# A third of the weight chunks split by an accumulating DMA in place of GpSimd arithmetic

## Chip, cores and metric

The kernel runs on one core of a Trainium2 chip, in one launch. The metric is the device time of that launch in microseconds; the time before is the median of three runs.

## The reference

A small decoder trunk over 512 tokens of width 1024, batch 1, in float32: one retention layer with four heads, then one multi-head latent attention layer with sixteen heads. Each has a SiLU gate, an output projection and a post-norm:

```
x = LN(alpha*x + retention_layer(x, a_w_in, a_w_out))
k_nope, k_rope, v = shared_latent_kv(x, kv_w_down, kv_norm, kv_w_up)
x = LN(alpha*x + mla_layer(x, b_w_in, q_norm, w_uq, b_w_out, k_nope, k_rope, v))
```

All work of weight is matrix products of activations (512 rows) with weights that are read once from HBM.

## The kernel before

**Three products for one.** TensorE multiplies float32r values. Each operand is split into a high part (`hi`, the value cast to float32r) and a low part (`lo`, the value less its high part), and `mm3` (L95) adds three products in a PSUM bank: high by high, and the two of a high with a low part (L97 to L99). So every weight chunk needs both parts before TensorE can finish with it.

**Weights.** All weights come as chunks of 128 rows and at most 1024 columns (512 KB), in the order in which they are used. That order is the list `order` in `trunk_kernel`. The class `Weights` (L37) works through it: `issue` (L51) loads a chunk from HBM into a stage buffer `wst` by a DMA on SyncE's queue, lets ScalarE cast it to `whi` (L66), and lets VectorE or GpSimd subtract `whi` from `wst` into `wlo` (L67, L68). One chunk in three goes to GpSimd: those with `n % 3 == 2`, after the first seven, whose names are not in `on_vector` (L44). `get` (L72) hands a chunk to TensorE and keeps two more issued ahead. High and low parts have four buffers each (pool `wpt`), so the cast of a chunk waits until TensorE has finished with the chunk four places earlier; stage buffers are eight in the retention layer and two in the second.

**Chunks made in place.** Per retention head, values and gates are computed by seven block products (`p1` to `p7`, fourteen chunks, `w_vg` at L110) in place of eight. Some of their weights are sums or differences of weight blocks, made in the stage buffers by VectorE or, for heads 1 to 3, by GpSimd (L118). Such a chunk is given as a function (`callable`) and not as an array in HBM.

**Order.** The recording layer orders the instructions of each engine itself when the program is built; each engine then works its queue strictly in that order and waits for semaphores. GpSimd's queue also has small reciprocal roots (`rsqrt`, L254 to L258) that the normalisations wait for.

**Stages.** Head by head: values and gates, the retention scores and their products (`inner`), transposes, output projection (`o0` to `o3`). After head 3 come the shared latent (`lat`), the query latent (`ql0`, `ql1`), then for sixteen heads in eight pairs the chunks `gb` (gate), `k`, `q`, `r` (rotary queries), `vb` (values) and `bo` (output), between which the attention work stands. One chunk of 1024 columns keeps TensorE busy for 24 products of 512 columns.

Of the kernel before, what the change touches and what calls it, by code (L numbers as in the profile page):

```python
# [8 lines left out]
F32 = mybir.dt.float32  # L9
BF16 = mybir.dt.bfloat16  # L10
F32R = mybir.dt.float32r
AF = mybir.ActivationFunctionType
ALU = mybir.AluOpType
# [15 lines left out]
EAGER = 7  # L29
# [7 lines left out]
class Weights:  # L37
# [13 lines left out]
    def issue(self, between=None):  # L51


        nc = self.nc
        name, aps, n = self.todo.pop(0)
        st = aps() if callable(aps) else self.stage.tile([P, WC], F32, tag="wst", name="wst")
        pool, th, tl = self.place[name].pop(0) if self.place.get(name) else (self.parts, "whi", "wlo")
        hi = pool.tile([P, WC], F32R, tag=th, name="whi")
        lo = pool.tile([P, WC], F32R, tag=tl, name="wlo")
        for j, ap in enumerate(aps if isinstance(aps, list) else [aps]):  # L60
            sl = slice(j * n, (j + 1) * n)
            if j and between:
                between()
            if not callable(ap):
                self.last = nc.sync.dma_start(st[:, sl], ap)
            nc.scalar.copy(hi[:, sl], st[:, sl])  # L66
            eng = nc.gpsimd if self.n % 3 == 2 and self.n > EAGER and name not in self.on_vector else nc.vector  # L67
            eng.tensor_tensor(out=lo[:, sl], in0=st[:, sl], in1=hi.bitcast(F32)[:, sl], op=ALU.subtract)  # L68
        self.n += 1
        self.ready.append((name, hi, lo))  # L70

# [1007 lines left out]
```

## Time and profile before

| | |
|---|---|
| median of the runs | 935.09 us (934.62 to 936.39) |
| the profiled execution | 934.96 us, of it span 933.2 us |
| TensorE busy | 914.1 us, 98% of the span |
| VectorE busy | 646.2 us, 69% |
| ScalarE busy | 357.2 us, 38% |
| GpSimd busy | 176.9 us, 19% |
| low parts on VectorE (L68) | 132 + 2, 1243 ns in the mean of the 132 |
| low parts on GpSimd (L68) | 49, 2264 ns in the mean |
| casts of weights on ScalarE (L66) | 181 + 2, 964 ns in the mean of the 181 |
| moved by DMA | 97.45 MB, 104 GB/s in the mean |

How to read it: busy time is the union of an engine's instructions, and products of TensorE overlap in it, so 98% does not mean that it works at its best rate; whether it waits is read from the gaps between the starts of its products. An engine that is busy for less than the span costs time only where another waits for it. DMA issues are not counted as busy time of the engine that issues them.

### The profile page before, as it was taken

To read this page: it belongs to the slowest core of one execution; us is meant where nothing else is said; L and a number is where in the kernel's file an instruction comes from. 1 tells how busy PE (TensorE), PEld (TensorE's weight loads), DVE (VectorE), ACT (ScalarE), POOL (GpSimd) and SP (SyncE) were. 2 spreads that over 40 slices of the span, in tenths; PEclk is the share of its full clock that TensorE was granted. 3 is DMA by queue.
4 is the path that set the end of the run, shared out by engine and by line. 5 is a ranking of instruction groups with operands and counts; after the bars stand their busy time and mean duration, and the time that the engine had idled before them with its cause. 6 is when DMAs were issued, how large, how long until landed. Compare 5 with 4: busy or idle time off the path is not lost.

```text
span 933.2 us, 11971 instructions
## 1 busy us (share of the span) xinstructions
PE 914.1 (98%) x4553; PEld 774.7 (83%) x4553; DVE 646.2 (69%) x1117; ACT 357.2 (38%) x600; POOL 176.9 (19%) x108
## 2 busy tenths in 40 slices
PE   9979999999999999999999999999999999999996
PEld 6758888888888887888988888888888888888885
DVE  7998767967696779963377576464864738657577
ACT  6453334333433345132535343333433334334431
POOL 0001126221641160112312011010011021111204
PEclk9989999999999999999999999999999999999998
DMA  9164204520352051234134424242242422423222
GB/s 333 61 224 138 90 12 141 175 78 25 136 180 72 30 187 40 68 87 136 52 116 108 121 76 118 75 126 72 74 122 76 125 68 74 127 78 107 91 68 91
DMA packets 32362, 97.45 MB, mean 104 GB/s; under 512 B 4272, under 2 KB 4912, under 8 KB 32304
## 3 DMA queue, kind: packets, MB, share of 16 engines
q1 hardware_dynamic: 28800, 87.11, 28.6%
q10 hardware_dynamic: 3504, 9.57, 4.1%
q8 instruction: 36, 0.59, 0.3%
q14 instruction: 22, 0.18, 0.1%
HBM read 86.18 MB, written 2.10 MB: 95 GB/s over the span
## 4 chain that ended last, share of the span: by engine, by line
PE 82%; DVE 8%; issue 4%; POOL 3%; DMA 2%; ACT 0%; SPq 0%; DVEq 0%; POOLq 0%; ACTq 0%
PE ps L98 26%; PE ps L99 26%; PE ps L97 25%; DVE wlo L68 2%; PE ps L839 2%; POOL wst L118 1%; PE ps L816 1%; PE ps L817 1%; DMA wst<-in_w_g 1%; DMA r<-in_xT 1%; DVE wst L118 1%; PE ps L531 1%; POOL wlo L68 1%; DMA cosA<-in_cosA 1%; PE ps L298 1%
## 5 line engine op out<-in xcount | busy, mean ns | idle before, releaser
L66 ACT CAST whi<-wst 128x1024 fp32r<-128x1024 f32 (+3 forms) x181 | 173.1, 964 | 266.7 <-PE ps L98 94.8
L68 DVE TENSOR_TENSOR wlo<-wst,whi 128x1024 fp32r<-128x1024 f32 (+2 forms) x132 | 163.5, 1243 | 98.6 <-ACT whi L66 98.3
L68 POOL TENSOR_TENSOR wlo<-wst,whi 128x1024 fp32r<-128x1024 f32 (+3 forms) x49 | 110.9, 2264 | 621.4 <-ACT whi L66 591.4
L824 ACT ACTIVATE p<-ps,sm 128x512 f32<-128x512 f32 (+1 forms) x64 | 33.4, 526 | 66.6 <-DVE sm L821 66.5
L97 PE MATMUL ps<-qlt_h,whi 128*128 128x512 f32 x144 | 56.9, 395 | 0.0
L98 PE MATMUL ps<-qlt_l,whi 128*128 128x512 f32 x144 | 56.5, 392 | 0.0
L99 PE MATMUL ps<-qlt_h,wlo 128*128 128x512 f32 x144 | 56.3, 391 | 0.0
L97 PE MATMUL ps<-x1h,whi 128*128 128x512 f32 x128 | 50.6, 395 | 0.0
L97 PE MATMUL ps<-whi,oTh 128*128 128x512 f32 x128 | 50.2, 392 | 0.0
L99 PE MATMUL ps<-whi,oTl 128*128 128x512 f32 x128 | 50.0, 390 | 0.1
L98 PE MATMUL ps<-x1l,whi 128*128 128x512 f32 x128 | 50.0, 391 | 0.0
L99 PE MATMUL ps<-x1h,wlo 128*128 128x512 f32 x128 | 49.9, 390 | 0.0
L98 PE MATMUL ps<-wlo,oTh 128*128 128x512 f32 x128 | 49.8, 389 | 0.0
L97 PE MATMUL ps<-whi,ogh 128*128 128x512 f32 (+1 forms) x114 | 44.7, 392 | 0.0
L99 PE MATMUL ps<-whi,ogl 128*128 128x512 f32 (+1 forms) x114 | 44.1, 387 | 0.0
L98 PE MATMUL ps<-wlo,ogh 128*128 128x512 f32 (+1 forms) x114 | 44.0, 386 | 0.0
L890 DVE TENSOR_TENSOR r<-r,ps 128x512 f32<-128x512 f32 (+1 forms) x49 | 32.4, 671 | 10.4 <-PE ps L99 10.4
L97 PE MATMUL ps<-xTh,whi 128*128 128x512 f32 x96 | 37.6, 392 | 0.0
L98 PE MATMUL ps<-wlo,xTh 128*128 128x512 f32 x96 | 37.5, 390 | 0.1
L99 PE MATMUL ps<-xTh,wlo 128*128 128x512 f32 x96 | 37.4, 389 | 0.0
L98 PE MATMUL ps<-xTl,whi 128*128 128x512 f32 x96 | 37.4, 389 | 0.0
L97 PE MATMUL ps<-whi,xTh 128*128 128x512 f32 x96 | 37.4, 389 | 0.0
(248 smaller groups left out, 2394.0 us busy)
## 6 DMA issues: line engine op xcount, KB each, us to landing
wst<-in_w_g SPq DMA_DIRECT2D x22, 512.0 KB, 3.3
wst<-in_w_v SPq DMA_DIRECT2D x16, 512.0 KB, 3.4
wst<-in_w_ao SPq DMA_DIRECT2D x16, 512.0 KB, 3.9
wst<-in_w_gb SPq DMA_DIRECT2D x16, 512.0 KB, 3.8
qr<-uv ACTq DMA_DIRECT2D x64, 128.0 KB, 2.4
wst<-in_w_bo SPq DMA_DIRECT2D x16, 512.0 KB, 3.6
wst<-in_w_qk SPq DMA_DIRECT2D x12, 512.0 KB, 3.9
wst<-in_w_q SPq DMA_DIRECT2D x16, 384.0 KB, 3.1
```

Source lines behind the costliest of these rows:

```text
L66: nc.scalar.copy(hi[:, sl], st[:, sl])
L68: eng.tensor_tensor(out=lo[:, sl], in0=st[:, sl], in1=hi.bitcast(F32)[:, sl], op=ALU.subtract)
L97: nc.tensor.matmul(ps, lhsT=lh, rhs=rh, start=start, stop=False)
L98: nc.tensor.matmul(ps, lhsT=lh, rhs=rl, start=False, stop=False)
L99: nc.tensor.matmul(ps, lhsT=ll, rhs=rh, start=False, stop=stop)
L118: eng.tensor_tensor(out=out, in0=x, in1=y, op=ALU.subtract)
L298: nc.tensor.transpose(out=ps[:, k * P : (k + 1) * P], in_=src[:, k * P : (k + 1) * P], identity=ident)
L531: nc.tensor.transpose(out=ps[:, k * P : (k + 1) * P], in_=gs[h][:, n, k * P : (k + 1) * P], identity=ident)
L816: nc.tensor.matmul(ps, lhsT=rh[:, qs], rhs=krp[:, :n], start=False, stop=False)
L824: nc.scalar.activation(pp, ps, AF.Exp, bias=sm[:, qb, 1:2], scale=SCALE_B, accum_out=sm[:, qb, 2:3])
L839: nc.tensor.transpose(out=ps[:, do : do + P], in_=pr[i][:, so : so + P], identity=ident)
L890: nc.vector.tensor_tensor(out=dst, in0=dst, in1=ps, op=ALU.add)
```

## The change

For chunks that are loaded from an array in HBM and that the rule gives to GpSimd, ScalarE now writes the negative of the high part into `wlo`, and a DMA issued from GpSimd's queue adds the chunk, read from HBM a second time, to what stands there. The load into the stage buffer stays, for the cast. Chunks made in place that GpSimd split before are split by VectorE.

```diff
-            eng = nc.gpsimd if self.n % 3 == 2 and self.n > EAGER and name not in self.on_vector else nc.vector
-            eng.tensor_tensor(out=lo[:, sl], in0=st[:, sl], in1=hi.bitcast(F32)[:, sl], op=ALU.subtract)
+            if self.n % 3 == 2 and self.n > EAGER and name not in self.on_vector and not callable(ap):
+
+                low = lo[:, sl]
+                nc.scalar.activation(low, hi.bitcast(F32)[:, sl], AF.Copy, scale=-1.0)
+                nc.gpsimd.dma_start(low, ap, accum_op=ALU.add)
+            else:
+                nc.vector.tensor_tensor(out=lo[:, sl], in0=st[:, sl], in1=hi.bitcast(F32)[:, sl], op=ALU.subtract)
```

Lines after the edit stand five further down in the changed kernel: L97 to L99 become L102 to L104, L118 becomes L123, L258 becomes L263. The copy is L70, the DMA L71, the subtraction L73. In the built program GpSimd has 37 such DMAs and no low part, ScalarE 37 copies more, VectorE 146 subtractions in place of 134.

The recording layer also orders some instructions anew. On GpSimd, in head 3 of the retention layer, the queue before was, from a chunk of head 2's output projection on (`wst<-wst` are the differences made in the stage buffers, `o_rs` the reciprocal roots):

```order
L68 TENSOR_TENSOR wlo<-wst,whi 128x1024 x3
L118 TENSOR_TENSOR wst<-wst 128x1024 x3
L68 TENSOR_TENSOR wlo<-wst,whi 128x1024
L118 TENSOR_TENSOR wst<-wst 128x1024
L258 TENSOR_TENSOR o_rs<-rs_t,mhalf 128x1 x4
```

and in the changed kernel it is:

```order
L71 DMA wlo<-in_w_ao 128x1024
L123 TENSOR_TENSOR wst<-wst 128x1024 x4
L263 TENSOR_TENSOR o_rs<-rs_t,mhalf 128x1 x4
```

Of the three low parts before the first difference one is now a DMA, the other two and the one before the last difference have gone to VectorE.

On TensorE, at the first chunk of `ql0` (`x1h`, `x1l` are the parts of the layer's input, `ident,latn` the transposes of the latent), before:

```order
L298 MATMUL ps<-ident,latn 128x128 x4
L97 MATMUL ps<-whi,x1h 128x512
L98 MATMUL ps<-wlo,x1h 128x512
L99 MATMUL ps<-whi,x1l 128x512
L97 MATMUL ps<-whi,x1h 128x512
```

and now:

```order
L303 MATMUL ps<-ident,latn 128x128 x4
L102 MATMUL ps<-whi,x1h 128x512 x4
L303 MATMUL ps<-ident,latn 128x128 x2
L103 MATMUL ps<-wlo,x1h 128x512
L104 MATMUL ps<-whi,x1l 128x512
```

Three more products with the high part and two transposes stand ahead of the first product with the low part.

On TensorE, at the second `gb` chunk, in the first pair of heads of the second layer (`ident,p` are the transposes of the softmax weights, `kn` and `qn` keys and queries without rotary part, `krp,qr` the rotary parts), before:

```order
L839 MATMUL ps<-ident,p 128x128 x10
L97 MATMUL ps<-x1h,whi 128x512
L98 MATMUL ps<-x1l,whi 128x512
L99 MATMUL ps<-x1h,wlo 128x512
```

and now:

```order
L844 MATMUL ps<-ident,p 128x128 x10
L102 MATMUL ps<-x1h,whi 128x512
L103 MATMUL ps<-x1l,whi 128x512
L102 MATMUL ps<-knh,qnh 128x512
L102 MATMUL ps<-knh,qnh 128x384
L102 MATMUL ps<-knh,qnh 128x256
L103 MATMUL ps<-knl,qnh 128x512
L104 MATMUL ps<-knh,qnl 128x512
L821 MATMUL ps<-krp,qr 128x512
L822 MATMUL ps<-krp,qr 128x512
L103 MATMUL ps<-knl,qnh 128x384
L104 MATMUL ps<-knh,qnl 128x384
L104 MATMUL ps<-x1h,wlo 128x512
```

Nine score products of the pair's other head now stand between the first two products of the gate and the first that reads its low part.

## Rows read from the trace of the kernel before

**Rows 1.** Windows, start:end, length, busy us of PE, PEld, DVE, ACT, POOL; clock, DMA share, GB/s.

```profile
340.00:360.00 20.00, 19.93 (x91) 16.28 (x91) 19.91 (x28) 10.87 (x15) 1.93 (x1) 1.00 0.53 180
360.00:380.00 20.00, 18.07 (x84) 14.15 (x83) 19.72 (x35) 7.10 (x10) 2.21 (x4) 1.00 0.09 23
600.00:620.00 20.00, 20.00 (x104) 17.14 (x103) 15.96 (x44) 7.91 (x19) 1.84 (x1) 1.00 0.34 96
```

**Rows 2.** Waits of TensorE: who for whom, us in total, times, longest us.

```profile
PE ps L97 <- ACT whi L66: 6.0, 1, 6.0
PE ps L531 <- DVE gs L520: 1.9, 2, 1.5
```

**Rows 3.** GpSimd's groups by form: busy us, mean ns, idle us before and releasers.

```profile
L68 POOL TENSOR_TENSOR wlo<-wst,whi 128x1024 fp32r<-128x1024 f32 x37 | 91.3, 2467 | 455.3 <-ACT whi L66 425.2 <-PE ps L817 14.4 <-DVE p L826 10.4
```

**Rows 4.** Timelines of VectorE and GpSimd, head 3: start us, us, instruction.

```profile
322.15 1.22 DVE L68 TENSOR_TENSOR wlo<-wst,whi 128x1024 fp32r<-128x1024 f32 x1
...
337.36 6.92 DVE L68 TENSOR_TENSOR wlo<-wst,whi 128x1024 fp32r<-128x1024 f32 x3 [4.54 <-ACT whi L66]
...
338.56 3.38 POOL L118 TENSOR_TENSOR wst<-wst 128x1024 f32<-128x1024 f32 x1
```

**Rows 5.** Timeline of TensorE at the end of head 3's inner products.

```profile
368.30 0.39 PE L98 MATMUL ps<-vl,sTh 128*128 128x512 f32 x1
368.52 0.39 PE L99 MATMUL ps<-vh,sTl 128*128 128x512 f32 x1
370.46 0.66 PE L531 MATMUL ps<-ident,gs 128*128 128x128 f32 x4 [1.54 <-DVE gs L520]
```

**Rows 6.** DMA issues (count, KB, median us to landing), whole run and 420:424; longest in chain.

```profile
wst<-in_w_g SPq DMA_DIRECT2D x22, 512.0 KB, 3.3
...
wst<-in_w_ql SPq DMA_DIRECT2D x2, 512.0 KB, 4.9
...
16.77 7.91 DMA wst<-in_w_g
```

**Rows 7.** GpSimd's short instructions with a wait, from the groups by form.

```profile
L258 POOL TENSOR_TENSOR o_rs<-rs_t,mhalf 128x1 f32<-128x1 f32 x16 | 8.8, 552 | 53.0 <-DVE rs_t L257 53.0
```

**Rows 8.** Timelines of ScalarE and TensorE at the first `ql0` chunk.

```profile
417.63 1.05 ACT L66 CAST whi<-wst 128x1024 fp32r<-128x1024 f32 x1 [0.66 <-PE ps L99]
...
421.54 0.60 PE L298 MATMUL ps<-ident,latn 128*128 128x128 f32 x4
421.89 0.48 PE L97 MATMUL ps<-whi,x1h 128*128 128x512 f32 x1
422.21 0.39 PE L98 MATMUL ps<-wlo,x1h 128*128 128x512 f32 x1
```

**Rows 9.** Timelines of ScalarE and TensorE at the first `vb` chunk.

```profile
476.49 1.05 ACT L66 CAST whi<-wst 128x1024 fp32r<-128x1024 f32 x1 [5.30 <-DMA wst<-in_w_vb]
...
482.75 0.28 PE L98 MATMUL ps<-wlo,lat_h 128*128 128x256 f32 x1
```

**Rows 10.** Timelines of ScalarE and TensorE at the second `gb` chunk.

```profile
495.92 1.05 ACT L66 CAST whi<-wst 128x1024 fp32r<-128x1024 f32 x1
496.86 0.59 ACT L102 CAST qnh<-ps 128x512 fp32r<-128x512 f32 x1
...
500.00 0.40 PE L99 MATMUL ps<-x1h,wlo 128*128 128x512 f32 x1
```

**Rows 11.** Timelines of ScalarE and TensorE at the third `gb` chunk.

```profile
510.25 0.47 ACT L824 ACTIVATE p<-ps,sm 128x256 f32<-128x256 f32 x1
...
518.56 0.40 PE L99 MATMUL ps<-x1h,wlo 128*128 128x512 f32 x1
```

**Rows 12.** Timelines of ScalarE and TensorE at the third `vb` chunk.

```profile
577.13 0.58 ACT L102 CAST qnh<-ps 128x512 fp32r<-128x512 f32 x1
...
587.48 0.28 PE L98 MATMUL ps<-wlo,lat_h 128*128 128x256 f32 x1
```

**Rows 13.** Window after TensorE's longest wait, columns as in rows 1.

```profile
60.60:66.40 5.80, 5.43 (x12) 3.84 (x13) 5.54 (x6) 3.81 (x5) 0.00 (x0) 0.50 0.50 150
```

## Prediction

> **What bounds the kernel now.** I read the windows of 20 us first, then the table of waits, then the timelines of the two places where TensorE does wait. In the windows TensorE is busy for all of nearly every slice [rows 1]: of 600 to 620 us it fills 20.00 us, while VectorE has 4, ScalarE 12 and GpSimd 18 us to spare. After the first 62 us, which the change leaves as they are (its condition holds from the 21st chunk on), only one stretch is different: from 340 to 380 us VectorE is busy for 39.63 us of 40, and TensorE falls to 18.07 us in the second half. The table of waits agrees [rows 2]: 6.0 us before the 62nd microsecond, 1.9 us behind the normalised gate `gs` of VectorE at about 370 us, and little else. So a faster preparation of weights can give back about 2 us and no more; a slower one costs whatever TensorE then waits for low parts. Those two sums decide.
>
> **What the change removes.** The order of GpSimd loses all 49 subtractions. The 37 of plainly loaded chunks become one negating copy on ScalarE and one accumulating DMA each; the other 12 belong to chunks that are made in place for heads 1 to 3 (5, 4 and 3 of them), and go to VectorE. A GpSimd subtraction of 1024 columns took 2.47 us [rows 3], one on VectorE alone 1.22 us [rows 4].
>
> For VectorE the 12 look like 12 x 1.22 = 14.6 us more, but the two engines hinder each other. In the saturated stretch three VectorE subtractions took 6.92 us together, where three undisturbed ones take 3.7, and GpSimd's own lasted 3.38 us meanwhile [rows 4]. GpSimd works there through two low parts (2.5 us each) among four subtractions of stage buffers, until 341.9 us. With the low parts gone its four end some 5 us earlier, at about 337 us, and the 3.2 us that VectorE lost to them are not lost in that stretch. The three low parts that VectorE gets in head 3 fall before it, where VectorE idles (4.54 us just before 337.36, in the same row), so they cost nothing; without that cover they would cost 3.7 us. VectorE then reaches `gs` about 3 us sooner. TensorE's steps there are 0.23 us, until one jumps from 368.52 to 370.46 [rows 5]: 1.71 us, most of the 1.9 us of the table. I take all **1.9 us** as gained, since 3.2 is more than the longest jump. The bounds are 0 (nothing shortened) and 1.9. Next in line behind `gs` is then TensorE itself. In heads 1 and 2 TensorE does not wait, so a freer VectorE gives nothing; the 9 extra subtractions there replace GpSimd subtractions that overlapped VectorE's work, and I take them at nothing too; without that exchange, the second rival has the price.
>
> **What the change adds.** On ScalarE, 37 copies of at most 1.05 us, the length of a cast of the same size [rows 8]: at most 39 us on an engine with 12 of 20 us free [rows 1]. Each is behind its cast or a few instructions after it. At most places the next instruction waits for TensorE longer than a copy lasts, or has microseconds of slack, so I cost them at nothing but for the delay to their own chunk, below. If that cover failed, each would cost up to 1.05 us.
>
> On the DMA engines, 37 reads of up to 512 KB. The HBM queue is at a third of its time in the slice from 600 us, and loads run well ahead of use: no cost. A stage buffer is even free 2.4 us earlier, since the low part no longer reads it; no TensorE wait hangs on that.
>
> On GpSimd, 37 issues that wait for the copies. Behind them stand small reciprocal roots and the stage subtractions; the order puts an issue where a 2.4 us subtraction stood, so nothing behind comes later, unless one issue takes longer than 2.4 us.
>
> **The term that decides** is how long after the negating copy a low part can be used. I call it X. No row shows a DMA that GpSimd issues, nor one that adds. The nearest from below is a plain 512 KB load from issue to landing, 3.3 us in the median; from above the longest load on the chain, 7.9 us among many at the start [rows 6]. An accumulating transfer has two inputs of 512 KB, the chunk and its negative. Two 512 KB loads in flight together took 4.9 us in the median [rows 6], the nearest row. I add 0.55 us for GpSimd to take it up, the length of its short instructions with a wait [rows 7]: **X = 5.5 us**, with ends at 3.3 and 7.9.
>
> The Trainium skill (DMA: Bandwidth & Descriptors, section "Anatomy of one DMA — SWDGE (gpsimd) path") fits a GpSimd-issued DMA as 2.0 us plus its bytes over 436 GB/s; an estimate from that page for 512 KB is 3.2 us, for a transfer that does not add. By it no low part would be late, and the sum would be that of the first rival; the two loads in flight together speak for a longer one.
>
> Before, a low part was ready about 2.5 us after its cast [rows 3]; now 1.05 + X = 6.6 us. I read for each of the 37 chunks when its cast ended and when TensorE first multiplied with its low part. The places with the least room are:
> - First `ql0` chunk: cast ends at 417.63 + 1.05 = 418.68, copy at 419.73. TensorE needed the low part at 422.21; the new order puts three more high products (0.23 each) and two transposes (0.09 each: four take 421.89 - 421.54) ahead, so 423.1 [rows 8]. Room 3.4 us, wait 5.5 - 3.4 = 2.1.
> - First `vb` chunk: cast ends at 477.54, copy at 478.59, needed at 482.75 [rows 9]. Room 4.2, wait 1.3.
> - Second `gb` chunk: cast ends at 496.97, then a `qnh` cast until 497.45, copy until 498.5; needed at 500.00, and the new order puts nine score products ahead (five of 512 columns, three of 384, one of 256, at 0.23 us for 512: 5 x 0.23 + 3 x 0.17 + 0.12 = 1.8), so 501.8 [rows 10]. Room 3.3, wait 2.2.
> - Third `gb` chunk: its copy stands behind an exp that ended at 510.72, so 511.8; needed at 518.56 [rows 11]. Room 6.8, no wait; at X = 7.9 it is 1.1.
> - Of the other 33 the third `vb` chunk has the least: its copy stands behind two casts, the last until 577.71, so 578.8; needed at 587.48 [rows 12]. Room 8.7, no wait.
>
> These waits add, for TensorE has no idle time behind them to catch up in: 2.1 + 1.3 + 2.2 = **5.6 us**. They are short enough not to touch the clock by the one comparison that the trace offers: after the wait of 6.0 us [rows 2] the granted clock was 0.50, the 1.2 GHz level, for 5.8 us in which 12 products took 5.43 us [rows 13] in place of 12 x 0.23 = 2.8; over the gap of 1.71 us it stayed at 1.00, which is 2.4 GHz [rows 1]. A fall costs 2.7 us by this; I take none.
>
> **Sum.** 934.96 (the profiled execution, 933.2 of it span) + 5.6 - 1.9 = **938.7 us**. The median of the runs is 935.09, 0.13 above that execution and well inside the terms' uncertainty.
>
> **Rivals.**
> 1. *The transfer is about as quick as a plain load, faster.* With X at 3.3 (the lower row) all rooms suffice, only the gain is left: 934.96 - 1.9 = 933.1. For it: plain loads show it. Against: it is one stream, and GpSimd adds its own step. Decides below X = 3.4. The skill's estimate belongs to this rival. Between X = 3.4 and 4.9 the three waits (3X - 10.9 where all three count) and the gain differ by less than 1.9 us: no change. Chance of X below 3.4: 0.10; of the stretch between: 0.28.
> 2. *VectorE becomes the bound in the heads.* If GpSimd's stage subtractions hinder it as before, three to five subtractions more per head land in saturated stretches: nothing gained in head 3 and about one subtraction (1.2 us) lost in each of heads 1 and 2, so 934.96 + 5.6 + 2.4 = 943.0. Against: the time of GpSimd's own low parts goes as well. Chance 0.10.
> 3. *The adding transfer is slow.* At X = 7.9: waits of 4.5 + 3.7 + 4.6 + 1.1 = 13.9, less 1.9: 947.0. Without the gain 948.9; a clock fall at each of the three longer waits would add 8.1 more. Chance 0.20.
> 4. *It does not do what it says.* The order shows 37 transfers and not 49, already counted; a chance of its own it has none.
>
> **How the numbers follow.** A measurement of this kernel can tell 0.2%, 1.9 us, from no change. My forecast, X from 4.9 to about 7, has 0.32; with rivals 2 and 3 slower has 0.62, same 0.28, faster 0.10. The range goes from rival 1, 933.1, to rival 3 without the gain, 948.9; a slower transfer and clock falls are left out. Slower cases alone would span 937 to 949.
>
> **What would show it.** In the new profile: GpSimd without any low-part subtraction and with DMA issues in their place; 37 negating copies of about 1 us on ScalarE; a landing of the added chunks some 5 us after issue; TensorE waiting for DMAs at the first `ql0`, the first `vb` and the second `gb` chunk, 1 to 2 us each, and nowhere in the later pairs of heads; the waits behind `gs` gone, VectorE's three subtractions near 337 us at 1.2 us each. The prediction is wrong if the landings take 3 us (no waits) or over 8, if TensorE waits in the later pairs, whose rooms I took as ample, or if the waits behind `gs` remain.

## The result, and the profile after

The changed kernel took 943.69 us in the median of four runs (941.17 to 945.53), the kernel before 935.58 beside it: a ratio of 1.0087, 95% interval 1.0063 to 1.0111. Slower, as forecast, but by 8 us and not by 3.6. A repeat with five runs (first experiment) gave 943.49 us and 1.0093 (1.0080 to 1.0106).

The first line of the page (busy time of each engine), and from its list of DMA queues the one that is new:

```profile
PE 916.9 (97%) x4553; PEld 776.4 (82%) x4553; DVE 646.7 (69%) x1129; ACT 391.0 (41%) x637; POOL 99.4 (11%) x96
...
q0 software_dynamic: 5328, 17.24, 10.9%
```

GpSimd lost 77 us of work, ScalarE gained 34, VectorE has what it had. The 77 are net: issuing a DMA counts as work in GpSimd's rows, 32 us for the 37. These transfers serve a fifth of the 183 weight casts, not a third; they moved 17.24 MB and held the DMA engines for 10.9% of the span. None of this says where 8 us went; the waits of TensorE do (for whom, total, times, longest, in us), in the profile of the first runs:

```profile
PE ps L102 <- ACT whi L66: 7.4, 1, 7.4
PE ps L103 <- DMA wlo<-in_w_ql: 3.9, 1, 3.9
PE ps L104 <- DMA wlo<-in_w_gb: 2.0, 1, 2.0
...
PE ps L103 <- DMA wlo<-in_w_vb: 1.1, 1, 1.1
...
PE ps L536 <- DVE gs L525: 0.3, 1, 0.3
```

The three waits for added low parts stand where the forecast put them, at the first `ql0`, the first `vb` and the second `gb` chunk. The wait for `gs` has shrunk from 1.9 us [rows 2] to 0.3. What answers to [rows 3] on GpSimd (busy us, mean ns, idle before), and the copy on ScalarE:

```profile
L123 POOL TENSOR_TENSOR wst<-wst 128x1024 f32<-128x1024 f32 x12 | 34.3, 2878 | 91.9 <-DVE wlo L73 91.8
...
L71 POOL DMA_DIRECT2D wlo<-in_w_gb x6 | 5.2, 863 | 99.0 <-ACT wlo L70 48.5 <-PE ps L104 20.6 <-DVE r L895 15.5
...
L70 ACT ACTIVATE wlo<-whi 128x1024 fp32r<-128x1024 f32 x25 | 26.6, 1062 | 0.4
```

No low part is subtracted on GpSimd any more, one issue of a DMA occupies it for 0.86 us, and a copy takes 1.06 us. The DMA issues (count, KB each, median us from issue to landing), an adding transfer and a load, which answer to [rows 6]:

```profile
wlo<-in_w_gb POOLq DMA_DIRECT2D x6, 512.0 KB, 6.1
...
wst<-in_w_ql SPq DMA_DIRECT2D x4, 512.0 KB, 4.3
```

And the windows of head 3, as in [rows 1]: TensorE is now busy for 19.61 us of the second one, where it had 18.07.

```profile
340.00:360.00 20.00, 20.00 (x97) 16.99 (x96) 19.95 (x28) 12.01 (x16) 1.41 (x1) 1.00 0.54 185
360.00:380.00 20.00, 19.61 (x92) 15.61 (x91) 19.77 (x35) 7.18 (x10) 2.21 (x4) 1.00 0.07 22
```

**Where the time went.** TensorE has no idle time to catch up in, so I took the start of its first product with each weight chunk in both traces and subtracted. The difference changes at few places only. In us, for the repeat of the changed kernel against the profile before:

| place | step | forecast |
|---|---|---|
| before 72 us | +0.3 | 0 |
| head 3 (340 to 372 us) | -2.1 | -1.9 |
| first `ql0` | +5.2 | +2.1 |
| first `vb` | +1.3 | +1.3 |
| second `gb` | +2.6 | +2.2 |
| third `gb` | +0.9 | 0 |
| all that follows (some 400 us) | -0.1 | 0 |
| sum | +8.1 | +3.7 |

The first profile has the same steps at head 3, `vb` and the second `gb`, 5.9 us at `ql0` and none at the third `gb`, and it has +2.6 us before 72 us, where no instruction of the change stands and the order is the same.

### The profile page after: what moved, and what is told of

It is laid out like the page before. It is cut to its first block, busy times and chain, and to the rows that moved or that the text cites. A ratio compares the mean times of both kernels' runs of the same rounds, so it can differ in the third digit from the quotient of the medians.

```text
span 943.7 us, 12011 instructions
## 1 busy us (share of the span) xinstructions
PE 916.9 (97%) x4553; PEld 776.4 (82%) x4553; DVE 646.7 (69%) x1129; ACT 391.0 (41%) x637; POOL 99.4 (11%) x96
## 3 DMA queue, kind: packets, MB, share of 16 engines
q0 software_dynamic: 5328, 17.24, 10.9%
## 4 chain that ended last, share of the span: by engine, by line
PE 81%; DVE 8%; DMA 4%; issue 3%; POOL 1%; ACT 1%; SPq 0%; DVEq 0%; POOLq 0%; ACTq 0%
PE ps L104 26%; PE ps L103 26%; PE ps L102 25%; DVE wlo L73 2%; PE ps L844 2%; PE ps L821 1%; PE ps L822 1%; DMA wst<-in_w_g 1%; DMA r<-in_xT 1%; DMA wlo<-in_w_ql 1%; DMA r<-in_x 1%; DVE wst L123 1%; PE ps L536 1%; POOL wst L123 1%; DMA wlo<-in_w_gb 1%
## 5 line engine op out<-in xcount | busy, mean ns | idle before, releaser
L73 DVE TENSOR_TENSOR wlo<-wst,whi 128x1024 fp32r<-128x1024 f32 (+2 forms) x144 | 176.2, 1228 | 92.5 <-ACT whi L66 85.4
L102 PE MATMUL ps<-qlt_h,whi 128*128 128x512 f32 x144 | 56.9, 395 | 0.0
L104 PE MATMUL ps<-qlt_h,wlo 128*128 128x512 f32 x144 | 56.3, 391 | 0.0
L104 PE MATMUL ps<-x1h,wlo 128*128 128x512 f32 x128 | 50.0, 391 | 2.0 <-DMA wlo<-in_w_gb 2.0
L102 PE MATMUL ps<-x1h,whi 128*128 128x512 f32 x128 | 50.6, 395 | 0.0
L102 PE MATMUL ps<-whi,oTh 128*128 128x512 f32 x128 | 50.2, 392 | 0.0
L104 PE MATMUL ps<-whi,oTl 128*128 128x512 f32 x128 | 50.0, 390 | 0.1
L102 PE MATMUL ps<-whi,ogh 128*128 128x512 f32 (+1 forms) x114 | 44.6, 392 | 0.0
L104 PE MATMUL ps<-whi,ogl 128*128 128x512 f32 (+1 forms) x114 | 44.1, 387 | 0.0
L123 POOL TENSOR_TENSOR wst<-wst 128x1024 f32<-128x1024 f32 x12 | 34.3, 2878 | 91.9 <-DVE wlo L73 91.8
L103 PE MATMUL ps<-wlo,x1h 128*128 128x512 f32 (+1 forms) x96 | 35.8, 373 | 3.9 <-DMA wlo<-in_w_ql 3.9
L102 PE MATMUL ps<-xTh,whi 128*128 128x512 f32 x96 | 37.6, 392 | 0.0
L104 PE MATMUL ps<-xTh,wlo 128*128 128x512 f32 x96 | 37.4, 389 | 0.0
L102 PE MATMUL ps<-whi,xTh 128*128 128x512 f32 x96 | 37.3, 389 | 0.0
```

The source lines that it names most:

```text
L73: nc.vector.tensor_tensor(out=lo[:, sl], in0=st[:, sl], in1=hi.bitcast(F32)[:, sl], op=ALU.subtract)
L102: nc.tensor.matmul(ps, lhsT=lh, rhs=rh, start=start, stop=False)
L103: nc.tensor.matmul(ps, lhsT=lh, rhs=rl, start=False, stop=False)
L104: nc.tensor.matmul(ps, lhsT=ll, rhs=rh, start=False, stop=stop)
L123: eng.tensor_tensor(out=out, in0=x, in1=y, op=ALU.subtract)
```

## The experiments

Each kernel was run beside the kernel before. The three lines at the heart of the change are called copy (L70), DMA (L71) and subtraction (L73).

**The changed kernel again.** No edit.

> The changed kernel once more, for its interval and for the 2.3 us by which TensorE stood later at 72 us in its first profile, ahead of any difference in the program. Theory A (those 2.3 us belong to that execution: the loads of r<-in_x landed late in it): in this profile TensorE at the 14th chunk stands within 1 us of the kernel before, ScalarE's first instruction on r begins near 55.9 us and not 57.8, and the time is 1.0065 to 1.008 of the kernel before. Theory B (the change costs them): again 2 to 2.5 us at 72 us, and 1.009 to 1.011. In both the three waits stand: 4 us at the first ql0, 1.2 at the first vb, 2.2 at the second gb.

Measured: 943.49 us, 1.0093 (1.0080 to 1.0106), above the range that theory A gave and in that of theory B. For the start theory A holds all the same: TensorE stood 0.3 us later at 72 us, and over the nine kernels that follow this figure lies between -1.1 and +0.9. In the first profile the loads of `r` landed late. Its rows, first the load, then ScalarE's first instruction on `r` and what it waited for:

```profile
r<-in_x SPq DMA_DIRECT2D x4, 512.0 KB, 6.7
...
57.81 1.06 ACT L567 ACTIVATE r<-r 128x1024 f32<-128x1024 f32 x1 [1.52 <-DMA r<-in_x]
```

and in the repeat:

```profile
r<-in_x SPq DMA_DIRECT2D x4, 512.0 KB, 5.9
...
56.15 1.06 ACT L567 ACTIVATE r<-r 128x1024 f32<-128x1024 f32 x1 [0.58 <-DMA r<-in_x]
```

The kernel before had 5.4 us there. So the 2.3 us belong to that execution, and from here on the repeat is the profile to read. Its waits have one more, a second one for `gb`:

```profile
PE ps L103 <- DMA wlo<-in_w_ql: 3.2, 1, 3.2
PE ps L104 <- DMA wlo<-in_w_gb: 2.6, 2, 2.0
...
PE ps L103 <- DMA wlo<-in_w_vb: 1.0, 1, 1.0
```

The first `ql0` chunk in the repeat, in the timelines of ScalarE, GpSimd and TensorE (start us, us, instruction, in brackets the idle time before and its releaser):

```profile
416.99 1.06 ACT L70 ACTIVATE wlo<-whi 128x1024 fp32r<-128x1024 f32 x1
...
418.35 0.89 POOL L71 DMA_DIRECT2D wlo<-in_w_ql  x1 [2.77 <-ACT wlo L70]
...
421.17 0.38 PE L303 MATMUL ps<-ident,latn 128*128 128x128 f32 x2
424.79 0.50 PE L103 MATMUL ps<-wlo,x1h 128*128 128x512 f32 x1 [3.24 <-DMA wlo<-in_w_ql]
...
425.66 0.63 PE L103 MATMUL ps<-wlo,x1h 128*128 128x512 f32 x1
426.09 0.63 PE L104 MATMUL ps<-whi,x1l 128*128 128x512 f32 x1
```

The copy ended at 418.05, GpSimd issued from 418.35 to 419.24, the data landed at 424.74: 6.7 us after the copy. And the wait is not all. Behind it the products start 0.43 us apart in place of 0.23. The windows behind this wait and behind that of the second `gb` (columns as in [rows 1]; the clock is the third number from the right):

```profile
425.60:428.60 3.00, 3.00 (x8) 2.32 (x7) 0.00 (x0) 2.10 (x2) 0.27 (x1) 0.50 0.65 213
509.20:512.20 3.00, 3.00 (x14) 2.49 (x15) 0.65 (x2) 0.29 (x2) 0.00 (x0) 1.00 1.02 294
```

After 3.2 us of waiting the granted clock was 0.50, the 1.2 GHz level; after 2.0 us it was 1.00, the 2.4 GHz level. Eight products at the lower level cost 1.6 us more. So the 5.2 us of this place are 3.4 to 3.5 of wait (start to start), 1.6 of clock and a little from the order.

**Only the twelve moved to VectorE.**

```diff
-                low = lo[:, sl]
-                nc.scalar.activation(low, hi.bitcast(F32)[:, sl], AF.Copy, scale=-1.0)
-                nc.gpsimd.dma_start(low, ap, accum_op=ALU.add)
+                nc.gpsimd.tensor_tensor(out=lo[:, sl], in0=st[:, sl], in1=hi.bitcast(F32)[:, sl], op=ALU.subtract)
```

> Only the twelve low parts of the chunks that are made in place go from GpSimd to VectorE; the 37 others stay GpSimd subtractions. Theory A (the gain at head 3 comes from GpSimd's twelve subtractions leaving, and VectorE has room for them): no wait at ql0, vb or gb, the waits for gs fall from 1.9 us to below 0.6, and the time is 0.997 to 0.9985 of the kernel before (-1.5 to -2.5 us), so faster than both. Theory B (the gain needs the 37 gone as well, since these share VectorE's way to SBUF): waits for gs stay at 1.5 to 2 us and the time is 0.999 to 1.001. Theory C (VectorE becomes the bound): 1.003 or more.

Measured: 933.92 us, 0.9983 (0.9974 to 0.9992): theory A, faster than both. Its table of TensorE's waits has no low part and no `gs`; these are its longest:

```profile
PE ps L102 <- ACT whi L66: 7.3, 1, 7.3
PE ps L244 <- DVE zero L241: 1.2, 1, 1.2
PE ps L102 <- ACT qkh L107: 1.1, 1, 1.1
```

**Only the 37 DMAs.**

```diff
-                nc.vector.tensor_tensor(out=lo[:, sl], in0=st[:, sl], in1=hi.bitcast(F32)[:, sl], op=ALU.subtract)
+                eng = nc.gpsimd if self.n % 3 == 2 and self.n > EAGER and name not in self.on_vector else nc.vector
+                eng.tensor_tensor(out=lo[:, sl], in0=st[:, sl], in1=hi.bitcast(F32)[:, sl], op=ALU.subtract)
```

> Only the 37 DMAs; the twelve low parts made in place stay on GpSimd. Theory A (the waits come from the DMAs alone, the gain of head 3 from the twelve): the three waits as in the changed kernel, 7 to 8.5 us in all with the slow clock behind the first, waits for gs near 1.9 us as before, and 1.008 to 1.011 of the kernel before. Theory B (the gain comes from the 37): waits for gs below 0.6 us and the same time as the changed kernel, 1.006 to 1.009.

Measured: 945.93 us, 1.0121 (1.0104 to 1.0138): theory A, a little above its range. Between 340 and 372 us TensorE gains nothing against the kernel before, and the wait for `gs` is back beside those for the DMAs:

```profile
PE ps L103 <- DMA wlo<-in_w_ql: 2.9, 1, 2.9
PE ps L104 <- DMA wlo<-in_w_gb: 2.9, 2, 2.1
PE ps L536 <- DVE gs L525: 1.9, 2, 1.5
```

The two halves of the change are thus apart: the twelve subtractions are the gain, the 37 DMAs the loss.

**Only the three of head 3.** The edit above (GpSimd subtracts in place of copy and DMA), with another condition:

```diff
-            if self.n % 3 == 2 and self.n > EAGER and name not in self.on_vector and not callable(ap):
+            if self.n % 3 == 2 and self.n > EAGER and name not in self.on_vector and not (callable(ap) and name.endswith(".3")):
```

> The kernel before with only the three low parts of head 3's chunks that are made in place moved from GpSimd to VectorE; the nine of heads 1 and 2 and the 37 others stay GpSimd subtractions. Theory A (the gain comes from these three alone, since GpSimd then makes its last chunk in head 3 about 2.8 us sooner; the nine others were worth nothing): TensorE 1.8 to 2.2 us earlier from head 3's products on, no wait for gs above 0.4 us, and 0.9975 to 0.9985 of the kernel before, as with all twelve. Theory B (the nine others give part of it): less than 1.2 us earlier, and 0.9985 to 1.000.

Measured: 932.68 us, 0.9970 (0.9958 to 0.9982), by the median the fastest kernel here and a little below theory A's range; its interval overlaps that of all twelve. The profiles are closer: between 340 and 372 us TensorE gains 2.4 us in this kernel and 2.4 in that of all twelve, and in both nothing changes from 72 to 340 us, the stretch of heads 1 and 2. So theory A holds, three subtractions carry the whole gain, though the step is a little over its 1.8 to 2.2 us. How they do it stands in the repeat of the changed kernel, whose three low parts of head 3 are on VectorE too (VectorE, GpSimd and ScalarE):

```profile
334.67 2.22 DVE L73 TENSOR_TENSOR wlo<-wst,whi 128x1024 fp32r<-128x1024 f32 x1
...
336.93 3.31 DVE L73 TENSOR_TENSOR wlo<-wst,whi 128x1024 fp32r<-128x1024 f32 x1
...
340.16 1.21 DVE L73 TENSOR_TENSOR wlo<-wst,whi 128x1024 fp32r<-128x1024 f32 x1
...
341.30 1.21 DVE L73 TENSOR_TENSOR wlo<-wst,whi 128x1024 fp32r<-128x1024 f32 x1
...
342.43 1.47 DVE L435 TENSOR_TENSOR sf<-ps,c 128x512 f32<-128x512 f32 x3
...
330.07 9.08 POOL L123 TENSOR_TENSOR wst<-wst 128x1024 f32<-128x1024 f32 x3 [1.56 <-DVE wlo L73]
...
339.19 1.05 ACT L66 CAST whi<-wst 128x1024 fp32r<-128x1024 f32 x1 [0.29 <-POOL wst L123]
```

In the kernel before:

```profile
344.20 1.48 DVE L430 TENSOR_TENSOR sf<-ps,c 128x512 f32<-128x512 f32 x3
...
341.97 1.06 ACT L66 CAST whi<-wst 128x1024 fp32r<-128x1024 f32 x1 [2.37 <-POOL wst L118]
```

GpSimd makes the head's last chunk by 339.15 us where it took until 341.94 [rows 4], so the last cast, the last low part and `sf` come earlier: `sf` by 1.8 us, or 2.1 with the 0.3 us by which this profile began late. VectorE is hindered as before while GpSimd works: two low parts took 2.22 and 3.31 us, and the two after 339.15 us took 1.21 each. It only starts on them 2.7 us sooner and has one done in what had been a wait. Where the DMAs stand beside this (the changed kernel and the five below that keep all or most of them), 0.3 us of wait for `gs` remain and the gain is 2.1 us; why was not tried.

**Copies without DMAs.** L71 is left out, so 37 low parts hold the negative high part; the addition of the chunk is not done.

> The changed kernel with ScalarE's 37 negative copies but no DMA behind them, so the 37 low parts hold the negative high part (the addition of the chunk is left out). Theory A (all the loss is the time from copy to landing; the copies cost nothing): no wait at ql0, vb and gb, and the gain of head 3 is kept: 0.997 to 0.9985 of the kernel before. Theory B (the copies delay ScalarE's other work by more than nothing): 1.001 or more, with waits for whi or for ScalarE's results that the kernel before does not have.

Measured: 933.24 us, 0.9971 (0.9960 to 0.9981): theory A. The 37 copies cost nothing, with GpSimd's 37 subtractions gone as well. In its profile TensorE gains 2.4 us at head 3 and 0.1 behind it, much as in the kernel of the twelve (at the start its TensorE stood 0.8 us ahead, that one's 0.8 behind), so emptying GpSimd further is worth nothing here.

**DMAs without the addition.** The chunk is loaded over the copy, which leaves the subtraction out.

```diff
-                nc.gpsimd.dma_start(low, ap, accum_op=ALU.add)
+                nc.gpsimd.dma_start(low, ap)
```

> The 37 DMAs from GpSimd without the addition: the chunk is loaded over its negative high part (the subtraction is left out). Theory A (the 5.5 us are issue and landing of a GpSimd DMA, whatever it does with the data): copy to landing within 0.5 us of the changed kernel's 5.4 to 5.9 us for 512 KB, and the same time within 1.5 us. Theory B (the addition costs, since each element must be read and written back): copy to landing 1.5 us shorter or more, near 3.5 to 4 us, the three waits shrink to 1 to 3 us in all, and 0.999 to 1.003 of the kernel before.

Measured: 937.11 us, 1.0021 (1.0010 to 1.0031): theory B by the time and the waits, though the transfer grew shorter by less than it said. From the end of the copy to the landing of 512 KB (25 transfers, each from its own rows) the median is 4.85 us, against 6.06 in the repeat of the changed kernel: the addition costs 1.2 us, 0.3 of them in the issue. The same bytes hold the DMA engines for 6.6% of the span, with the addition for 11.3%. First the kernel without the addition:

```profile
q0 software_dynamic: 5328, 17.24, 6.6%
wlo<-in_w_gb POOLq DMA_DIRECT2D x6, 512.0 KB, 4.8
```

and the repeat of the changed one:

```profile
q0 software_dynamic: 5328, 17.24, 11.3%
wlo<-in_w_gb POOLq DMA_DIRECT2D x6, 512.0 KB, 6.3
```

The wait at `ql0` is 1.6 us then, and the clock behind it stays at 1.00:

```profile
422.40:425.40 3.00, 3.00 (x14) 2.44 (x14) 0.72 (x1) 1.64 (x2) 0.00 (x0) 1.00 0.50 160
```

**One chunk back, three chunks back.** The first `ql0` chunk (the 93rd, `n` = 92) is subtracted on GpSimd again; then also the first `vb` and the second `gb` chunk (`n` = 104, 107). The edit of the second kernel, whose other branch gives these chunks to GpSimd:

```diff
-            if self.n % 3 == 2 and self.n > EAGER and name not in self.on_vector and not callable(ap):
+            if self.n % 3 == 2 and self.n > EAGER and name not in self.on_vector and not callable(ap) and self.n not in (92, 104, 107):
```

> One of the 37 low parts, that of the first ql0 chunk, is GpSimd's subtraction again; the other 36 come by DMA. Theory A (that chunk costs its wait of 4.1 us and the slow clock behind it, 5.5 to 6 us less what is made up later): 5 to 6 us faster than the changed kernel, 1.002 to 1.004 of the kernel before, with no wait at ql0. Theory B (the DMA engines are the limit in that stretch, and the wait moves to the next chunk's transfer): a wait for the next DMA'd chunk or for its successor's load appears, and the gain is under 3 us.

Measured: 940.25 us, 1.0045 (1.0028 to 1.0063), 4.5 us less than the changed kernel by the ratios, just under theory A. The step at `ql0` is gone entirely and no later load takes its place, as theory A says. But the second `gb` costs 4.5 us in this profile in place of 2.6: TensorE waited 2.21 us, and the clock fell there. This execution took 941.25 us and the fastest 937.66, so whether the clock fell in each is open. TensorE's timeline, and the window behind:

```profile
504.85 0.79 PE L104 MATMUL ps<-x1h,wlo 128*128 128x512 f32 x1 [2.21 <-DMA wlo<-in_w_gb]
...
505.20:508.20 3.00, 3.00 (x8) 2.32 (x8) 0.56 (x2) 0.00 (x0) 0.00 (x0) 0.50 1.02 330
```

> Three of the 37 low parts, those of the first ql0, the first vb and the second gb chunk, are GpSimd's subtractions again; the other 34 come by DMA. Theory A (these three transfers are the whole loss): no wait for a low part by DMA above 0.3 us, and 0.997 to 1.000 of the kernel before. Theory B (the loss sits in the other DMAs too, or moves to the next chunk): 1.003 or more.

Measured: 934.60 us, 0.9991 (0.9982 to 0.9999): theory A by the time. One wait for a DMA is left, above the 0.3 us that theory A allowed, at the third `gb`:

```profile
PE ps L104 <- DMA wlo<-in_w_gb: 0.5, 1, 0.5
```

So three of 37 transfers are nearly all of the loss. A fourth costs 0.8 us here (start to start), and the other 33 show no wait of TensorE.

**The stage buffer held.** One GpSimd instruction of one column reads the chunk's stage buffer and low part, so the next load into that buffer cannot start before the transfer is done. (The line that makes `tiny` is left out here.)

```diff
                 nc.gpsimd.dma_start(low, ap, accum_op=ALU.add)
+                if self.n == 92: nc.gpsimd.tensor_tensor(out=self.tiny, in0=st[:, 0:1], in1=lo.bitcast(F32)[:, 0:1], op=ALU.subtract)
```

> The changed kernel, and behind the accumulating DMA of the first ql0 chunk one GpSimd instruction of one column that reads this chunk's buffer and its low part: the buffer is then given back only after the transfer, and the next load into it starts later. Theory A (that transfer took 7.4 us and not 5.5 because the next load, issued earlier than in the kernel before, shares the DMA engines with it): copy to landing falls to 5.5 to 6 us there, the wait from 4.1 to 2.1 to 2.7 us, no slow clock behind it, and 2.5 to 3.5 us faster than the changed kernel. Theory B (the 7.4 us have another cause): still 7 us or more, and the same time as the changed kernel within 1 us, or slower by what the late load costs.

Measured: 943.19 us, 1.0087 (1.0073 to 1.0101). The transfer is theory A's: 5.7 us from copy to landing, and a wait of 2.3 us. SyncE's loads of `ql0` in the repeat begin before GpSimd's issue at 418.35 (start, length of the group):

```profile
416.98 10.32 SPq L65 DMA_DIRECT2D wst<-in_w_ql  x4
```

and here after the one at 418.51:

```profile
420.43 7.72 SPq L65 DMA_DIRECT2D wst<-in_w_ql  x3
...
423.99 0.50 PE L103 MATMUL ps<-wlo,x1h 128*128 128x512 f32 x1 [2.29 <-DMA wlo<-in_w_ql]
```

So a load that came early did slow this transfer, by about 1 us: without the hold it took 6.4 to 7.4 us in four profiles. The second transfer of `ql0` took 7.2 us here and 5.6 to 5.8 there, without a wait of TensorE. But the forecast of 2.5 to 3.5 us fails, since the clock fell all the same:

```profile
424.80:427.80 3.00, 3.00 (x8) 2.32 (x7) 1.23 (x1) 1.04 (x1) 0.00 (x0) 0.50 0.60 183
```

The step at `ql0` is 4.3 us in place of 5.2, too little for the medians to tell.

**Low parts read last.** All DMAs stay; TensorE takes the products with the high part of four chunks first (first `ql0`, first `vb`, second and third `gb`). Of the edit only the new helper is shown, not the places that call it.

```diff
+    def mm3_late(items, side):
+        for ps, l, r, start, stop in items:
...
+            nc.tensor.matmul(ps, lhsT=lh, rhs=rh, start=start, stop=False)
+            x = (ll, rh) if side else (lh, rl)
+            nc.tensor.matmul(ps, lhsT=x[0], rhs=x[1], start=False, stop=False)
+        for ps, l, r, start, stop in items:
...
+            x = (lh, rl) if side else (ll, rh)
+            nc.tensor.matmul(ps, lhsT=x[0], rhs=x[1], start=False, stop=stop)
```

> The changed kernel, all 37 DMAs in place, but TensorE reads four low parts (first ql0, first vb, second and third gb) after its products with the high part: 16 products of 512 columns go first at ql0 and gb, 16 of 256 at vb. Theory A (the room between copy and first use decides, and the transfers are no worse elsewhere): the first use comes 2.4 us later at ql0, 1.9 at vb, 1.3 at the second gb and 3.2 at the third, so the waits shrink to 0 to 1, 0, 0.5 to 1 and 0 us, the clock stays at 1.00 behind ql0, and the time is 0.998 to 1.001 of the kernel before. Theory B (the transfers hold up other loads too, so that the wait moves to another chunk): 1.004 or more, with waits for low parts elsewhere.

Measured: 936.92 us, 1.0017 (1.0009 to 1.0026), 7 us better than the changed kernel by the ratios and just above theory A's range.

TensorE's waits for DMAs:

```profile
PE ps L115 <- DMA wlo<-in_w_gb: 1.8, 2, 1.2
...
PE ps L115 <- DMA wlo<-in_w_ql: 1.0, 1, 1.0
```

The wait at `vb` is gone, that at `ql0` is at the upper end of what was expected and that at the second `gb` 0.2 us above it, and the clock stays at 1.00 behind both. The third `gb`, expected without a wait, kept its 0.6 us: ScalarE took that chunk's copy at 514.09, 1.4 us after its cast and behind other work, and the transfer took 8.0 us. Room decides, but in a fixed order the room moves too.

## Why the prediction was right, and where it fell short

The time lies in the range that was given, and the mechanism is the one forecast: waits at three named places, less a gain at head 3. The loss is 8.1 us by the profiles and not 3.7, and 3.1 of the 4.4 us between them stand at the first `ql0`.

- **Gain at head 3, -1.9: right in size, half right in cause.** The changed kernel gains 2.1 and three subtractions are the cause. But the prediction had GpSimd done at about 337 us, some 5 us earlier, and VectorE's low parts there at 1.2 us each. GpSimd was done at 339.15, 2.8 us earlier, for its differences wait for VectorE in turn (1.56 us before 330.07), and two of VectorE's low parts took 2.2 and 3.3. VectorE gains by an earlier start, not by being undisturbed. The bound of 1.9 was 0.2 too low: 0.36 us of the gain stand at 352 us, where TensorE used a low part as soon as VectorE had made it, a wait that its table does not list. The nine other subtractions at nothing: shown.
- **X, 5.5 us: right as a middle, wrong as one number.** Between 5.4 and 8.8 us for the 25 transfers of 512 KB, 5.7 in the median in the first profile and 6.1 in the repeat. GpSimd starts its issue 0.3 us after the copy and takes 0.9, where I had 0.55; from the end of the issue the data took 4.6 to 4.9 us in the median, where the estimate has the 4.9 of two loads in flight. That an adding transfer lasts as long because it is like two loads is not shown, so this agreement may be luck. The estimate from the Trainium skill (DMA: Bandwidth & Descriptors, "Anatomy of one DMA — SWDGE (gpsimd) path"), 3.2 us for 512 KB that are not added, is exceeded even without the addition: 4.85 us from the end of the copy, 4.0 from the end of the issue. The measurement decides.
- **First `vb` and second `gb`: right** (1.3 and 2.6 for 1.3 and 2.2); their X was 5.7 to 5.9.
- **First `ql0`, 2.1 us: the step that failed, twice.** The transfer took 6.7 us (7.4 in the first profile). I had noted that a stage buffer is free 2.4 us earlier and that no wait hangs on it; the load which that sets off early is in flight beside this transfer, which took 5.7 us with that load held back. And "a fall costs 2.7 us by this; I take none": the clock fell and cost 1.6 us, here and even with the wait of 2.3 us of the held buffer. With that wait shortened to what I forecast, the place still cost 4.3.
- **Third `gb`, no wait: off by 0.9 in the repeat, right in the first profile.** I said that there is room for 6.8 us and that it waits 1.1 at X = 7.9; X was 7.7 in the repeat and 6.8 in the first profile. Loads of `gb`, `q` and `k` were in flight beside it; that they are the cause was not tried.
- **ScalarE's copies at nothing, later pairs without waits: right,** shown by the copies alone and by the last row of the table.

Rivals: the quick transfer fell, even unadded transfers make TensorE wait; VectorE did not become the bound; the slow transfer made TensorE wait at two places only, with one fall of the clock.

## What to carry to other kernels

Taking work off an engine with time to spare gains only where another waits for that engine's next result: three of 49 low parts carried the gain, and no further relief of GpSimd added to it here. A cheap operation replaced by a slower one costs at the few places with the least room between producer and first reader; list these places, give each its own duration by what else is in flight there, and leave them on the fast path or read their result last. Price the slow clock behind a wait of TensorE as a case of its own.

## What the runs showed of the hardware

- A DMA with addition issued by GpSimd held the DMA engines 1.7 times as long as the same DMA without (11.3% against 6.6% of the span for 17.24 MB), and its issue took GpSimd 0.86 us against 0.53 in the median.
- Pauses of TensorE of 0.8 us and more behind 72 us, in all profiles, and the granted clock after them: 0.8 to 1.2, 1.5, 1.64 and 2.01 to 2.05 us with 1.00 after; 2.21, 2.29, 2.9, 3.2 and 3.9 us with 0.50 after, for 7 to 9 products. The pauses of 2.01 to 2.05 us (four profiles) and that of 2.21 us are at the same place, the second `gb`. What separates them was not tried.
- A GpSimd subtraction of 1024 columns slows VectorE's beside it: 2.2 and 3.3 us beside it in head 3, 1.21 each right after it.
